# A two-layer mixer encoder on one core: where convolution's matmuls stand in the mixer, and behind what the weights at the stage joints are split

## The chip, the core and the metric

The kernel runs on one core of one Trainium2 chip. The metric is the device time of one execution in microseconds (us). A core has five engines, each with its own instruction stream: TensorE (PE) multiplies matrices, VectorE (DVE) and ScalarE (ACT) work elementwise, GpSimd (POOL) does a few small steps, SyncE (SP) issues most DMAs. An engine takes its instructions in the order in which they were put into its stream, and waits at the head of the stream until what the instruction needs is there. So the order of each stream, which is fixed when the kernel is built, decides what can hide what.

## What is computed

The reference is a two-layer encoder over 256 tokens of width 1024. Cut to what matters here:

```python
for l in range(DEPTH):                      # DEPTH = 2
    g = norm_g[l]
    h = rms_norm(x, g[0])
    x = x + 0.5 * rms_norm(swiglu(h, ffn_w_gate[l, 0], ffn_w_up[l, 0], ffn_w_down[l, 0]), g[1])
    h = rms_norm(x, g[2])
    z = h @ w_in[l]
    ...
    y = jnp.concatenate([y_conv, y_ret, y_rwkv, y_mlstm], axis=-1) @ w_out[l]
    x = x + rms_norm(y, g[3])
    h = rms_norm(x, g[4])
    x = x + 0.5 * rms_norm(swiglu(h, ffn_w_gate[l, 1], ffn_w_up[l, 1], ffn_w_down[l, 1]), g[5])
```

`swiglu(h, g, u, d)` is `(silu(h @ g) * (h @ u)) @ d` with 2816 inner columns. The four mixers are a short convolution, a retention scan, an RWKV-7 scan in both directions and an mLSTM, each 256 columns wide. All is float32.

## The kernel before, in words

**Stages.** The stages run in the order f00, m0, f01, f10, m1, f11: an FFN, the mixers and an FFN for each of the two layers (the digits of f are layer and place; m has the layer). There are four kinds of joints: FFN to mixer (f00 to m0, f10 to m1), mixer to FFN (m0 to f01, m1 to f11), FFN to FFN (f01 to f10), and the end behind f11.

**Weights.** All weights stream in elements of 128x1024 float32 (0.5 MB). `Stream.next` (L242 to L262) takes a raw tile from a pool of four, issues its DMA on SP's queue, then splits the element: ScalarE copies it to `hi` (rounded to the type that TensorE takes at full rate), VectorE subtracts to get `lo`. The first four elements of a stage are split in halves (`SPLITC`). Each product is made of three matmuls, hi by hi, hi by lo and lo by hi (`TERMS`). A raw tile comes free when its lo is done, and only then can the DMA of a later element that is given that tile start; SP issues its DMAs in order.

**An FFN** (`ffn`, L399). The 22 blocks `fb` of 128 inner columns need three elements each: a and b (gate and up, `fetch_ab`) and d (down, `fetch_d`). In the stream the order is a0 b0 a1 b1 a2 b2 d0 d1 d2, then a b d for each block; so element 6 is d0. `block` makes `pg` (L472, L474), the gating steps `gu`, and `hT` (hi on ScalarE, lo on VectorE at L488); `rows` makes the products `y` (L495) with the d element, for both token halves 0 and 1 (`tk`). For the last seven blocks (`NEPI`) the rows of token half 1 are kept back and stand behind all rows of token half 0, so that they cover the norm of token half 0: `resid` (`jk` squares on ScalarE, `yg`, `x` on VectorE) and `norm_t` (`jk`, `r_n` on POOL, `xg`, then `pt`, the transposes on TensorE at L314, and `XT`, the next stage's input, hi and lo). `turn()` emits the transposes and the XT writes.

**The mixers** (`mixers`, L560). The input projection gives z_in, q, k and v tiles; `conv` makes convolution's three projections, 6 elements, 24 matmuls of 128x256 each (`pz`, L388). The rwkv part is a generator: first it inverts small triangular blocks ("merge": 32x32 matmuls `pe`, L937 to L985), then runs the chain over chunks (`pakv`, `pu`, `psn`, `oT`, `pwc`), up to `pm` (L1065). mLSTM is a second generator (`pmb`, `pss`, `pom`). At the end stand 96 matmuls of the output projection (`ym`, L1334), in which two token halves take turns as in the FFN, and `ptf` (L786), the transposes of a mixer's output.

**What sets the order.** Each generator yields an estimate of the TensorE time of what it has just emitted. The loop at the end of `mixers` runs rwkv and, when the time of rwkv times a ratio is ahead of the time filled in, takes steps of the filler: `RATIO` with `fill1`, from "quads" (the merge) on `RATIO2` with `fill2`. Within `fill2`, `mix(a, b, R2)` puts convolution's steps between those of the retention output and mLSTM in the same way, and mLSTM's own estimate (`yield 0.22`) counts. A scheduler then places the instructions on the engines.

**Holds.** `held(*ins)` lets what is emitted inside stand on its engine only behind the instructions given, where they are on the same engine; it is an order, not a wait for another engine. `ffn` returns a table for the next stage, from element number to the instructions behind which its split stands: before, the elements 1 to 3 (2 and 3 ahead of a mixer) stood behind `done[1:]`, the lo half of the last `hT` on VectorE. `mixers` returned None, so the split of the next FFN's elements was free, and `fetch_ab` used `hold is None` to know that it follows a mixer.

Of the kernel before, what the change touches and what calls it, by code (L numbers as in the profile page):

```python
# [22 lines left out]
NFB = DFF // P  # L23
# [82 lines left out]
def tile_encoder(ctx: ExitStack, tc: tile.TileContext, x_in, wffn, win, wout, gains, params, idn, cst, rel, out, dbg=None):  # L106
# [286 lines left out]

    TA, TB, TC, SG = 4, 2, 7, 2
    NPRO, NEPI, SPLITC, WARM, W_FIN, ZW = 3, 7, 4, 6, 6.0, 2
    RATIO, RATIO2, W_PREP, W_INV, GRAIN, R1, R2, WQ, QG, KD = 0.8, 0.6, 8, 12, 0.8, 1.4, 1.2, 0.12, 8, 2

    def ffn(hold, l, j, XT, before1, before2, ahead, after, first, last, mix_next):

        st = Stream(wffn[l, j], f"f{l}{j}_", hold, first)  # L400
        ws, hts, nb = {}, {}, [0]

        def fetch_ab(fb):
            m = (m4, m4)
            new = m if fb == 2 or (fb == 1 and hold is None) else None
            ws[fb] = [st.next(new)]

            def second(ends=None):
                if ends:
                    st.hold[1] = ends  # L410
                ws[fb].append(st.next(new))
                return st.halves[0]

            if before1 and fb == 0:
                before1(second)
            else:
                second()
# [82 lines left out]
        turn = None  # L500
        hh = []
        for fb in range(NPRO):
# [4 lines left out]
            if fb == 0:  # L507
                turn = before2()
# [5 lines left out]
        y = ytiles(f"y{l}{j}")  # L514
# [26 lines left out]
        for fb in range(fb0, NFB - 4):  # L541
# [3 lines left out]
            if fb == fb0 + 3:  # L545
                mid = early + (st.dma,)
# [7 lines left out]

        for fb in range(NFB - 3, NFB):
            fetch_ab(fb)
            fetch_d(fb)
            done = block(fb)
        ahead(2)
        for fb in range(NFB - 4, NFB - 1):  # L560
            rows([fb], 0)
        end0 = rows([NFB - 1], 0)
        turn = after(0, y[0])
        with held(end0):
            for n, fb in enumerate(range(NFB - NEPI, NFB - SG)):
                rows([fb], 1)
                if n == TA and turn:
                    turn()
            rows(range(NFB - SG, NFB), 1)
        return y, {i: done[1:] for i in range(2 if mix_next else 1, 4)}, mid  # L570


    def split_out(dst, src_ps):
# [3 lines left out]
    def mixers(hold, l, XT, before2, ahead, after):  # L577
# [217 lines left out]
        hold = {}  # L795
# [365 lines left out]
        def mlstm():  # L1161
# [8 lines left out]
            for d in range(2):  # L1170
                for hp in range(2):
                    pm_ = ps.tile([P, 2, S], F32, tag="a", bufs=PA, name="pmb")
                    for i in range(2):
                        j = 4 * d + 2 * hp + i
                        T.matmul(pm_[:, i, :], lhsT=pair[64:128, j:j + 1].broadcast_to([64, P]), rhs=MR[64:128, d, :],
                                 start=i == 0, stop=True, skip_group_check=True)
                    yield 0.22
                    if d == 0 and hp == 0:
                        pc = ps.tile([P, 2, 16], F32, tag="o", bufs=1, name="pc")
                        for tk in range(2):  # L1180
                            T.matmul(pc[:, tk, :], lhsT=gT[:, tk * P:(tk + 1) * P], rhs=c_("sel"), start=tk == 0, stop=True,
                                     skip_group_check=True)
                        V.tensor_copy(out=cc, in_=pc[:, :, 0:8])
                        act(em, pc[:, :, 8:16], AF.Exp, scale=-1.0)
                    for i in range(2):
                        h = 2 * hp + i
                        j = 4 * d + h
                        for sk in range(2):
                            t0 = toff[d][sk]
                            act(wf[d][sk][:, h, :], pm_[:, i, t0:t0 + tn[d][sk]], AF.Exp, scale=-1.0,  # L1190
                                             bias=cc[:, sk, j:j + 1])
# [137 lines left out]
        y = [[], []]  # L1329
# [51 lines left out]
        for i in (4, 5):  # L1381
            for h in range(2):
                wo_rows(i, 1, h)
        turn()
        for h in range(2):
            for i in (6, 7):
                wo_rows(i, 1, h)
        return y, None


    seq = []
# [139 lines left out]
```

## Time and profile before

| what | us |
| --- | --- |
| median of three runs | 1164.4 |
| the three runs | 1164.4, 1154.44, 1165.07 |
| the profiled execution | 1157.71 |
| its span in the profile | 1156.0 |

The profile is of one execution; 1.71 us of it lie outside the span. In the rows that the prediction shows, a line of the timeline is start, duration, engine, line of the kernel, operation, output from input, shape and count; in square brackets stands how long the engine had been idle before it, and what released it. Matmuls are pipelined: a matmul of 128x512 is shown as 0.39 us long, but they start 0.23 us apart. The tables by stretch give the busy time of PE, PEld, DVE, ACT and POOL with the number of instructions, then the mean granted clock of TensorE (1.00 is full), the share of DMA time and GB/s.

### The profile page before, as it was taken

How to read it: one execution, taken by the hardware profiler on the slowest of the kernel's cores; microseconds unless marked ns; L12 is line 12 of the kernel's file. 1: busy time of each engine (PE TensorE's matmuls, PEld its weight loads, DVE VectorE, ACT ScalarE, POOL GpSimd, SP SyncE). 2: the span in 40 equal slices, each digit the busy share in tenths (PEclk: the TensorE clock that was granted, in tenths of full speed). 3: DMA queues.
4: the chain of work that ended last, by engine and by line, in shares of the span. 5: the costliest groups of instructions: out<-in, count | busy, mean ns of one | idle time of the engine just before them, and what ended most of it. 6: DMA issues, size and time to landing. Idle time of an engine off the chain costs nothing.

```text
span 1156.0 us, 20352 instructions
## 1 busy us (share of the span) xinstructions
PE 1116.3 (97%) x8083; PEld 954.3 (83%) x8083; DVE 787.4 (68%) x1371; ACT 653.5 (57%) x1193; POOL 51.4 (4%) x87
## 2 busy tenths in 40 slices
PE   8999999999899999999899999999989999999997
PEld 6888887897878788888798888879868778888886
DVE  6666566798867856566666656667895578566663
ACT  7575555777435755454555555568764157555562
POOL 0000000012000000000000000000301000000000
PEclk9999999999999999999999999999998799999999
DMA  7856554432323666655546655625242136665641
GB/s 259 278 188 202 181 189 157 145 125 90 114 72 108 202 222 193 203 174 199 179 149 207 215 186 186 209 73 185 74 159 63 56 127 205 204 196 185 197 163 37
DMA packets 53535, 189.46 MB, mean 164 GB/s; under 512 B 6200, under 2 KB 6848, under 8 KB 53440
## 3 DMA queue, kind: packets, MB, share of 16 engines
q1 hardware_dynamic: 51120, 181.28, 47.8%
q10 hardware_dynamic: 2320, 6.89, 1.8%
q8 instruction: 63, 1.03, 0.3%
q14 instruction: 32, 0.26, 0.1%
HBM read 187.10 MB, written 1.05 MB: 163 GB/s over the span
## 4 chain that ended last, share of the span: by engine, by line
PE 60%; DVE 12%; DMA 12%; ACT 8%; issue 6%; POOL 1%; SPq 0%; POOLq 0%; ACTq 0%; DVEq 0%
PE pg L472 16%; PE y L495 14%; DMA f_raw<-in_wffn_dram 11%; PE pz L388 9%; PE pg L474 8%; DVE f_lo L259 4%; ACT f_hi L142 4%; PE pgh L444 2%; DVE i_lo L259 1%; PE pss L1097 1%; PE pvg L594 1%; PE ym L1334 1%; ACT i_hi L142 1%; ACT jk L142 1%; DVE gu L121 1%
## 5 line engine op out<-in xcount | busy, mean ns | idle before, releaser
L259 DVE TENSOR_TENSOR f_lo<-f_raw,f_hi 128x1024 fp32r<-128x1024 f32 (+1 forms) x280 | 323.0, 1162 | 195.6 <-ACT f_hi L142 194.9
L472 PE MATMUL pg<-XT,f_hi 128*128 128x512 f32 x1232 | 387.4, 396 | 1.4 <-DVE gu L121 1.3
L142 ACT ACTIVATE f_hi<-f_raw 128x1024 fp32r<-128x1024 f32 (+1 forms) x280 | 279.0, 1007 | 137.8 <-DMA f_raw<-in_wffn_dram 116.6
L474 PEld LDWEIGHTS pg<-XT,f_lo 128*128 128x128 f32 x1232 | 231.3, 188 | 54.0
L474 PE MATMUL pg<-XT,f_lo 128*128 128x256 f32 x1232 | 242.2, 278 | 0.0
L495 PE MATMUL y<-f_hi,hT 128*128 128x512 f32 x704 | 232.6, 392 | 3.8 <-ACT hT L142 2.7
L472 PEld LDWEIGHTS pg<-XT,f_hi 128*128 128x128 f32 x1232 | 192.6, 189 | 7.4 <-DVE gu L121 2.2
L495 PEld LDWEIGHTS y<-f_hi,hT 128*128 128x128 f32 x704 | 131.6, 188 | 31.0 <-ACT hT L142 4.0
L388 PE MATMUL pz<-XT,i_hi 128*128 128x256 f32 x704 | 139.8, 295 | 2.2 <-DVE rvg L121 1.4
L495 PE MATMUL y<-f_lo,hT 128*128 128x512 f32 x352 | 137.3, 391 | 0.0
L388 PEld LDWEIGHTS pz<-XT,i_hi 128*128 128x128 f32 x704 | 111.4, 193 | 10.3 <-issue 4.1
L142 ACT ACTIVATE hT<-gu 128x256 fp32r<-128x256 f32 x77 | 32.1, 417 | 130.8 <-DVE gu L121 130.8
L388 PE MATMUL pz<-XT,i_lo 128*128 128x256 f32 x352 | 101.3, 288 | 0.0
L259 DVE TENSOR_TENSOR i_lo<-i_raw,i_hi 128x1024 fp32r<-128x1024 f32 (+1 forms) x68 | 73.6, 1095 | 14.5 <-ACT i_hi L142 13.5
L142 ACT ACTIVATE i_hi<-i_raw 128x1024 fp32r<-128x1024 f32 (+1 forms) x68 | 63.5, 953 | 34.4 <-PE pz L388 22.8
L121 DVE TENSOR_TENSOR gu<-pg,gu 128x256 f32<-128x256 f32 x154 | 64.4, 418 | 16.1 <-ACT gu L142 16.1
L495 PEld LDWEIGHTS y<-f_lo,hT 128*128 128x128 f32 x352 | 66.1, 188 | 11.1 <-DVE f_lo L259 0.4
L444 PE MATMUL pgh<-f_hi,XT 128*128 128x256 f32 x352 | 69.0, 290 | 2.1 <-ACT XT L142 1.1
L388 PEld LDWEIGHTS pz<-XT,i_lo 128*128 128x128 f32 x352 | 68.0, 193 | 0.8 <-issue 0.5
L142 ACT ACTIVATE gu<-pg 128x256 f32<-128x256 f32 x154 | 56.8, 369 | 18.7 <-PE pg L474 18.7
L444 PEld LDWEIGHTS pgh<-f_hi,XT 128*128 128x128 f32 x352 | 56.6, 191 | 5.3 <-ACT XT L142 1.8
L488 DVE TENSOR_TENSOR hT<-gu,hT 128x256 fp32r<-128x256 f32 x77 | 32.8, 425 | 35.1 <-ACT hT L142 34.5
(290 smaller groups left out, 1275.7 us busy)
## 6 DMA issues: line engine op xcount, KB each, us to landing
f_raw<-in_wffn_dram SPq DMA_DIRECT2D x262, 512.0 KB, 4.4
i_raw<-in_win_dram SPq DMA_DIRECT2D x60, 512.0 KB, 4.0
o_raw<-in_wout_dram SPq DMA_DIRECT2D x16, 512.0 KB, 3.7
gain<-in_gains_dram ACTq DMA_DIRECT2D x11, 512.0 KB, 4.9
x<-in_x_dram SPq DMA_DIRECT2D x4, 256.0 KB, 4.3
f_raw<-in_wffn_dram SPq DMA_DIRECT2D x4, 256.0 KB, 5.1
rl<-in_rel_dram ACTq DMA_DIRECT2D x2, 384.0 KB, 3.2
C<-in_cst_dram SPq DMA_DIRECT2D x1, 573.0 KB, 6.9
```

Of the source, the lines that this page charges most:

```text
L121: eng.tensor_tensor(out=out, in0=a, in1=b, op=op)
L142: return A.activation(out, a, f, **kw)
L259: V.tensor_tensor(out=lo[:, cs], in0=r[:, cs], in1=f(hi[:, cs]), op=ALU.subtract)))
L388: T.matmul(dst, lhsT=w[a][:, k * P:(k + 1) * P], rhs=xt(XT, k, b), start=n == 0, stop=n == 23)
L444: T.matmul(pg, lhsT=xt(XT, k, a)[:, tk * P:(tk + 1) * P], rhs=w[b][:, c:c + 256], start=n == 0, stop=n == 23)
L472: T.matmul(pg, lhsT=w[0][:, c:c + P], rhs=xt2(XT, k + i), start=k + i == 0, stop=False, skip_group_check=True)
L474: T.matmul(pg[:, 0, :], lhsT=w[1][:, c:c + P], rhs=xt(XT, k + i, 0), start=False, stop=k + i == 7, skip_group_check=True)
L488: V.tensor_tensor(out=hT[:, 1, :], in0=h, in1=f(hT[:, 0, :]), op=ALU.subtract))
L495: ins = T.matmul(y[tk][h], lhsT=hts[fb][:, a, tk * P:(tk + 1) * P], rhs=ws[fb][2][b][:, h * 512:(h + 1) * 512], start=fb == 0 and i == 0, ...
L594: T.matmul(pv[tk], lhsT=xt(XT, k, a)[:, tk * P:(tk + 1) * P], rhs=w[b][:, (k % 2) * 512:(k % 2 + 1) * 512], start=k == 0 and i == 0, stop= ...
L1097: T.matmul(pq[hp][:, p, :], lhsT=t[half[hp], 2 + p, sk * P:(sk + 1) * P], rhs=t[half[hp], p, :], start=p == 0, stop=True, skip_group_check ...
L1334: T.matmul(y[tk][h], lhsT=yT[(1, 0, 3, 2)[i // 2]][:, a, i % 2, tk * P:(tk + 1) * P], rhs=wo[i][b][:, h * 512:(h + 1) * 512], start=i == 0 ...
```

## The change

It has three parts.

1. Three numbers of the mixer's planner: `RATIO2` 0.6 to 0.75, `R2` 1.2 to 1.45, and mLSTM's yield from 0.22 to 0.5.
2. The last d element of each FFN is fetched and split behind the last block, held behind both halves of its `hT` (before it was fetched ahead of that block).
3. The holds at the joints. FFN to FFN: element 2 behind the last hT's lo, elements 3 and 4 behind `ends`, the last XT writes of token half 0 (`turn()` now hands them out). FFN to mixer: elements 2 and 3 as before. Mixer to FFN, free before: element 2 behind the two steps that scale `xg`, element 3 behind `ends`. The key "mix" takes the place of the test for None.

```diff
@@ -393,7 +393,7 @@
 
     TA, TB, TC, SG = 4, 2, 7, 2
     NPRO, NEPI, SPLITC, WARM, W_FIN, ZW = 3, 7, 4, 6, 6.0, 2
-    RATIO, RATIO2, W_PREP, W_INV, GRAIN, R1, R2, WQ, QG, KD = 0.8, 0.6, 8, 12, 0.8, 1.4, 1.2, 0.12, 8, 2
+    RATIO, RATIO2, W_PREP, W_INV, GRAIN, R1, R2, WQ, QG, KD = 0.8, 0.75, 8, 12, 0.8, 1.4, 1.45, 0.12, 8, 2
 
     def ffn(hold, l, j, XT, before1, before2, ahead, after, first, last, mix_next):
 
@@ -402,7 +402,7 @@
 
         def fetch_ab(fb):
             m = (m4, m4)
-            new = m if fb == 2 or (fb == 1 and hold is None) else None
+            new = m if fb == 2 or (fb == 1 and "mix" in hold) else None
             ws[fb] = [st.next(new)]
 
             def second(ends=None):
@@ -554,8 +554,12 @@
 
         for fb in range(NFB - 3, NFB):
             fetch_ab(fb)
-            fetch_d(fb)
+            if fb < NFB - 1:
+                fetch_d(fb)
             done = block(fb)
+
+        st.hold[st.i] = done
+        fetch_d(NFB - 1)
         ahead(2)
         for fb in range(NFB - 4, NFB - 1):
             rows([fb], 0)
@@ -565,9 +569,9 @@
             for n, fb in enumerate(range(NFB - NEPI, NFB - SG)):
                 rows([fb], 1)
                 if n == TA and turn:
-                    turn()
+                    r = turn()
             rows(range(NFB - SG, NFB), 1)
-        return y, {i: done[1:] for i in range(2 if mix_next else 1, 4)}, mid
+        return y, {2: done[1:], 3: done[1:] if mix_next or last else r[1], 4: () if mix_next or last else r[1]}, mid
 
 
     def split_out(dst, src_ps):
@@ -1174,7 +1178,7 @@
                         j = 4 * d + 2 * hp + i
                         T.matmul(pm_[:, i, :], lhsT=pair[64:128, j:j + 1].broadcast_to([64, P]), rhs=MR[64:128, d, :],
                                  start=i == 0, stop=True, skip_group_check=True)
-                    yield 0.22
+                    yield 0.5
                     if d == 0 and hp == 0:
                         pc = ps.tile([P, 2, 16], F32, tag="o", bufs=1, name="pc")
                         for tk in range(2):
@@ -1381,11 +1385,12 @@
         for i in (4, 5):
             for h in range(2):
                 wo_rows(i, 1, h)
-        turn()
+        r = turn()
         for h in range(2):
             for i in (6, 7):
                 wo_rows(i, 1, h)
-        return y, None
+
+        return y, {"mix": True, 2: r[0], 3: r[1]}
 
 
     seq = []
```

What it does to the order is not seen in the diff. Three places, as the rows stand on an engine; a name's number at its end tells one tile from another, and behind f00_, i0_, o0_ stand the stage's stream, hi, lo or raw, and the element's number.

ScalarE at the joint f00 to m0, before (hT_1830 is the last block's hT, i0 the mixer's stream, jk the first step of the norm):

```order
L142 ACTIVATE gu_1826<-pg_1809 128x256
L142 ACTIVATE hT_1830<-gu_1805 128x256
L142 ACTIVATE i0_hi3_1992<-i0_raw3_1990 128x512 x2
L142 ACTIVATE jk_1862,st3_1861<-y00_00_317 128x512
L142 ACTIVATE jk_1864,st3_1861<-y00_01_318 128x512
```

and after (f00_hi65 is the last d element):

```order
L142 ACTIVATE gu_1820<-pg_1803 128x256
L142 ACTIVATE hT_1824<-gu_1799 128x256
L142 ACTIVATE f00_hi65_1829<-f00_raw65_1827 128x1024
L142 ACTIVATE i0_hi3_1992<-i0_raw3_1990 128x512 x2
L142 ACTIVATE jk_1862,st3_1861<-y00_00_317 128x512
```

The last d element's copy moved in between the last hT and the norm. On VectorE its lo moved in the same way, between the lo halves of the mixer's elements 2 and 3:

```order
L488 TENSOR_TENSOR hT_1824<-gu_1799,hT_1824 128x256
L259 TENSOR_TENSOR i0_lo2_1985<-i0_raw2_1982,i0_hi2_1984 128x512 x2
L259 TENSOR_TENSOR f00_lo65_1830<-f00_raw65_1827,f00_hi65_1829 128x1024
L259 TENSOR_TENSOR i0_lo3_1993<-i0_raw3_1990,i0_hi3_1992 128x512 x2
L121 TENSOR_TENSOR yg_1866<-y00_00_317,gain0_1_671 128x512
```

VectorE at the joint f01 to f10, ahead of the norm's first step yg, before:

```order
L488 TENSOR_TENSOR hT_5972<-gu_5947,hT_5972 128x256
L259 TENSOR_TENSOR f10_lo1_6100<-f10_raw1_6097,f10_hi1_6099 128x512 x2
L259 TENSOR_TENSOR f10_lo2_6163<-f10_raw2_6160,f10_hi2_6162 128x512 x2
L259 TENSOR_TENSOR f10_lo3_6171<-f10_raw3_6168,f10_hi3_6170 128x512 x2
L121 TENSOR_TENSOR yg_6008<-y01_00_4472,gain0_5_4888 128x512
```

and after:

```order
L488 TENSOR_TENSOR hT_5966<-gu_5941,hT_5966 128x256
L259 TENSOR_TENSOR f10_lo2_6163<-f10_raw2_6160,f10_hi2_6162 128x512 x2
L259 TENSOR_TENSOR f01_lo65_5972<-f01_raw65_5969,f01_hi65_5971 128x1024
L121 TENSOR_TENSOR yg_6008<-y01_00_4472,gain0_5_4888 128x512
L139 SCALAR_TENSOR_TENSOR st3_6003<-st3_6003 128x1
```

Elements 1 and 3 left the place ahead of yg, and f01's last d element came to stand there.

TensorE between the merge and the chain in m0, before (pe5 is the merge's last step, pakv the chain's first, pmb and pc are mLSTM's, pz is convolution's):

```order
L997 MATMUL pakv_3526<-UV0_2624,GP01_2530 64x64
L388 MATMUL pz_3495<-XT0_21_1834,i0_lo26_3499 128x256
L388 MATMUL pz_3495<-XT0_21_1834,i0_hi26_3498 128x256 x2
L985 MATMUL pe5_3415<-D64T_3191,F__3413 32x32 x31
L388 MATMUL pz_3495<-XT0_21_1834,i0_lo26_3499 128x256
L997 MATMUL pakv_3526<-UV0_2624,GP00_2516 64x64
L1175 MATMUL pmb_3490<-MR_3405,pair_85 128x256 x2
```

and after:

```order
L388 MATMUL pz_3551<-XT0_20_1833,i0_hi27_3554 128x256
L1179 MATMUL pmb_3478<-MR_3432,pair_85 128x256 x2
L1179 MATMUL pmb_3490<-MR_3432,pair_85 128x256 x2
L388 MATMUL pz_3551<-XT0_20_1833,i0_hi27_3554 128x256
L388 MATMUL pz_3551<-XT0_20_1833,i0_lo27_3555 128x256
L1001 MATMUL pakv_3535<-UV0_2624,GP00_2516 64x64
L1001 MATMUL pakv_3535<-UV0_2624,GP01_2530 64x64
```

The four pz next to pe5 x31 moved forward: six pz now stand ahead of pe5's first row (not shown) and six (three, one and two) between it and these last rows; behind them come pakv, pc, pe5 x31 and pmb without a pz, then six pz.

## The prediction

> **What bounds the kernel now.** I read the page's busy times first, then a table by stage with the granted clock, then the timeline of TensorE for its idle times, then the other engines' rows beside those.
>
> The first line of the page (engine, busy us, share, instructions):
>
> ```profile
> PE 1116.3 (97%) x8083; PEld 954.3 (83%) x8083; DVE 787.4 (68%) x1371; ACT 653.5 (57%) x1193; POOL 51.4 (4%) x87
> ```
>
> TensorE is busy 1116.3 of 1156.0 us. No edit takes a matmul away, so the change can only move the 40 us in which TensorE is not busy, or the clock at which it is. The same work of the two mixers, the end of the merge and the rwkv chain, in stretches (PE, PEld, DVE, ACT, POOL busy; then the granted clock):
>
> ```profile
> 311.00:350.50 39.50, 39.50 (x645) 32.02 (x639) 25.03 (x63) 14.76 (x41) 2.59 (x6) 1.00 0.27 82
> 876.10:927.20 51.10, 51.10 (x642) 40.06 (x638) 25.90 (x64) 14.84 (x42) 2.46 (x4) 0.73 0.22 64
> 882.50:885.00 2.50, 2.50 (x73) 2.06 (x71) 1.23 (x1) 2.48 (x9) 0.00 (x0) 1.00 0.23 26
> 885.00:887.50 2.50, 2.50 (x32) 2.18 (x31) 0.69 (x1) 1.81 (x6) 1.23 (x2) 0.53 0.51 190
> 887.50:910.00 22.50, 22.50 (x152) 15.62 (x150) 7.91 (x21) 4.29 (x11) 1.23 (x2) 0.50 0.00 1
> 910.00:912.50 2.50, 2.50 (x19) 2.05 (x16) 1.61 (x4) 0.07 (x1) 0.00 (x0) 0.51 0.02 7
> 912.50:915.00 2.50, 2.50 (x60) 2.23 (x62) 1.89 (x6) 0.64 (x3) 0.00 (x0) 1.00 0.00 0
> ```
>
> Layer 0 takes 39.5 us, layer 1 51.1 us for as many matmuls. From 885 to 912.4 the clock is at half, and that costs 51.1 − 39.5 = 11.6 us. It is the largest thing here that the change can touch: the runs lie between 1154.4 and 1165.1, which is about one such stretch apart. What stands ahead of the drop, in layer 0 at full clock:
>
> ```profile
> 314.56 0.40 PE L388 MATMUL pz<-XT,i_hi 128*128 128x256 f32 x2
> ...
> 316.58 0.62 PE L1181 MATMUL pc<-C,gA 128*128 128x16 f32 x4
> ...
> 317.50 0.38 PE L388 MATMUL pz<-XT,i_lo 128*128 128x256 f32 x1
> 317.72 0.40 PE L388 MATMUL pz<-XT,i_hi 128*128 128x256 f32 x2
> 318.05 1.19 PE L985 MATMUL pe<-D64T,F__3413 32*32 32x32 f32 x62
> 319.17 0.38 PE L388 MATMUL pz<-XT,i_lo 128*128 128x256 f32 x1
> ...
> 319.74 0.50 PE L1175 MATMUL pmb<-MR,pair 64*128 64x256 f32 x2
> 320.17 1.03 PE L997 MATMUL pakv<-UV,GP 64*64 64x64 f32 x28
> ...
> 322.04 0.51 PE L388 MATMUL pz<-XT,i_hi 128*128 128x256 f32 x2
> ```
>
> Layer 1's clock drops where layer 0 is at about 319.9. From 314.96, the end of the first row, to 322.04, 7.1 us, only four of convolution's 128x256 matmuls run (pz); most of the rest are 32x32 and 64x64 pieces.
>
> **The change part by part.**
>
> *Convolution spread (RATIO2, R2, 0.5).* The same 144 matmuls move from behind pm to between the merge's and the chain's. By the order, six pz now stand ahead of pe5's first row, six more among the first pakv and pmb, then comes one stretch with none: 20 rows of pakv (two matmuls each, 40 at 1.03/28 = 0.037, 1.5 us), pc (0.6), pe5 (318.05 to 319.17, 1.1) and one pmb row (319.74 to 320.17, 0.4), together 3.6 us, then 6 pz and soon 14. With four pz allowed as before, the thin stretch is some 5 us long in place of 7.1 (two pmb rows, four of pakv and four pz more). So a drop becomes rarer, not impossible. I take the value without a drop, −11.6 us against the profiled run, and keep 0 as the other end. The merge's own waits:
>
> ```profile
> 301.06 0.25 PE L949 MATMUL pe<-En,DT 32*32 32x32 f32 x5 [0.42 <-DVE En L943]
> 302.01 0.37 PE L949 MATMUL pe<-En,DT 32*32 32x32 f32 x22 [0.70 <-issue]
> ...
> 868.40 0.38 PE L949 MATMUL pe<-En,DT 32*32 32x32 f32 x21 [0.74 <-issue]
> ```
>
> More pz in front of pe cover a wait for VectorE; what "issue" is, no row shows. Of 0.42 + 0.70 + 0.74 = 1.9 I take half, −0.9 (bounds −1.9 and 0). The 36 pz that stood behind pm covered the end of the chain; now ym stands there, 96 matmuls at 0.23, 22 us, and its weights stand ahead of it on ScalarE and VectorE. I cost that at nothing; were o's first weights late, pm's tail would show.
>
> *Last d element behind the last block, before a mixer.* The place in the timelines:
>
> ```profile
> 179.05 0.50 PE L472 MATMUL pg<-XT,f_hi 128*128 128x512 f32 x1 [0.77 <-DVE gu L121]
> 177.58 1.04 ACT L142 ACTIVATE f_hi<-f_raw 128x1024 fp32r<-128x1024 f32 x1
> 178.92 1.22 DVE L259 TENSOR_TENSOR f_lo<-f_raw,f_hi 128x1024 fp32r<-128x1024 f32 x1
> 188.93 0.42 ACT L142 ACTIVATE hT<-gu 128x256 fp32r<-128x256 f32 x1 [0.95 <-DVE gu L121]
> 189.38 0.43 DVE L488 TENSOR_TENSOR hT<-gu,hT 128x256 fp32r<-128x256 f32 x1 [0.48 <-ACT hT L142]
> 189.72 2.49 DVE L259 TENSOR_TENSOR i_lo<-i_raw,i_hi 128x512 fp32r<-128x512 f32 x4
> 189.40 0.50 PE L495 MATMUL y<-f_hi,hT 128*128 128x512 f32 x1 [0.40 <-ACT hT L142]
> 197.69 1.03 PE L314 MATMUL pt<-ident,xg 128*128 128x128 f32 x8
> 755.39 0.50 PE L495 MATMUL y<-f_hi,hT 128*128 128x512 f32 x1 [0.40 <-ACT hT L142]
> ```
>
> Early, one hi (1.04) and one lo (1.22) go from in front of gu, so the 0.77 wait at 179.05 goes and hT comes at about 188.6 in place of 189.35. Late, the last six y of token half 0 need the element. ScalarE copies it behind hT (to 189.6). VectorE does hT lo (0.34), the two halves of the next stage's element 2 (half of 2.49, 1.25) and then f_lo (1.22), done at 188.6 + 0.34 + 1.25 + 1.22 = 191.4. Four of the six y wait for that and take 0.9, so they end at 192.3; before, six from 189.40 at 0.23 each end at 190.8. That is +1.6 us. Layer 1 has no 0.77 to win: +2.3. Behind f_lo on VectorE stand element 3's lo and yg, behind f_hi on ScalarE element 3's hi and jk: about 1.2 us later each, but pt at 197.69 moves with TensorE by 1.6, so the norm is no new wait. Element 3's DMA no longer reuses the last ab slot but the one of the next stage's element 0, whose lo stands eleven rows earlier on VectorE; I take it as in time. Sum +3.9 (bounds 0, if VectorE's backlog in the mixer swallows it, and +4.6).
>
> *The same at the end of the last FFN.* Nothing of a next stage stands between:
>
> ```profile
> 1136.04 0.42 ACT L142 ACTIVATE hT<-gu 128x256 fp32r<-128x256 f32 x1 [0.95 <-DVE gu L121]
> 1139.41 0.60 ACT L142 ACTIVATE jk<-y 128x512 bf16<-128x512 f32 x1 [2.96 <-PE y L495]
> ```
>
> The last six y end at 1139.4, so they begin at 1138.0 and the first lo among them at 1138.2; f_lo is done at 1136.46 + 1.05 + 1.22 = 1138.7. +0.5 (0 to 1.2).
>
> *FFN to FFN.*
>
> ```profile
> 562.12 1.06 ACT L142 ACTIVATE f_hi<-f_raw 128x1024 fp32r<-128x1024 f32 x1 [1.63 <-DMA f_raw<-in_wffn_dram]
> 565.26 0.42 ACT L142 ACTIVATE hT<-gu 128x256 fp32r<-128x256 f32 x1 [1.81 <-DVE gu L121]
> 566.05 3.69 DVE L259 TENSOR_TENSOR f_lo<-f_raw,f_hi 128x512 fp32r<-128x512 f32 x6
> 565.73 0.50 PE L495 MATMUL y<-f_hi,hT 128*128 128x512 f32 x1 [1.94 <-ACT hT L142]
> 576.04 0.41 PE L314 MATMUL pt<-ident,xg 128*128 128x128 f32 x2 [1.85 <-DVE xg L301]
> ```
>
> Element 4's copy no longer holds up the last gu for its DMA, so hT comes about 2 us earlier; then the d element's lo takes as long as the 1.94 did. Of the six half lo (3.69) ahead of yg two stay, with one whole lo (1.22), all 2 us earlier: the norm gains about 2, and pt's 1.85 goes. But elements 3 and 4 are now split behind the turn, and the second half of element 3's lo stands on VectorE behind the other token half's whole norm; TensorE reaches it about 1.5 us too early. Sum 0 (−1.9 to +1.9).
>
> *Mixer to FFN, twice.*
>
> ```profile
> 363.73 0.44 PE L786 MATMUL ptf<-ident,og 128*128 128x128 f32 x2 [1.15 <-DVE og L121]
> 383.14 0.33 PE L314 MATMUL pt<-ident,xg 128*128 128x128 f32 x1 [1.75 <-DVE xg L301]
> 396.08 0.49 PE L495 MATMUL y<-f_hi,hT 128*128 128x512 f32 x1 [0.78 <-ACT f_hi L142]
> ...
> f_raw<-in_wffn_dram SPq DMA_DIRECT2D x262, 512.0 KB, 4.4
> ```
>
> ptf now stands behind more than 36 ym, which cover its 1.15. pt moves behind all ym, the halves of elements 2 to 4 go from in front of it on VectorE, and its wait stays near 1.7. Element 2 now waits for the scaled xg, so its slot comes free later, and d0, whose DMA waits for that slot (4.4 us to land), makes the 0.78 about 2.2; element 3's late half adds some 0.75. −1.15 + 1.4 + 0.75 = +1.0 each, +2.0 (bounds −2.3, nothing late, and +7.2, a landing uncovered each time: 4.4 − 0.78).
>
> *Sum* against the profiled execution's 1157.7: −0.9 + 3.9 + 0.5 + 0 + 2.0 = +5.5, 1163.2 with one half-clock stretch as in that execution; −11.6 without, **1151.6**. The profiled execution is 6.7 below the median of the runs, 1164.4, as if that median had more of the half clock.
>
> [...] In the rows above, TensorE is busy 2.50 of 2.50 us just ahead of the drop, and the half clock lasts 27.4 us. [...]
>
> **The rivals.**
> 1. *The drop stays in one layer*: the 3.6 us without any pz are longer than a gap of before, such as 319.55 to 322.04. Against it: twelve pz stand closely ahead, six behind. 1163.2.
> 2. *It comes in both layers*, as the median above hints: 1163.2 + 11.6 = 1174.8.
> 3. *The joints do what they are changed for* and nothing is late: all terms at their good bounds, no drop: 1157.7 − 11.6 − 1.9 + 0 + 0 − 1.9 − 2.3 = 1140.0. Against it: the reuse of slots and the order.
> 4. *Slower*: the half clock, once entered, is kept to the end of the chain in each layer, since pz come in ones to fives there and a dense stretch comes only with ym. The 27.4 us at half cost 11.6, so they held 15.8 us of work: 0.73 us for each. From 319.9 to pm at 350.5 are 30.6 us of work, 22.5 us a layer: 1151.6 + 45 = 1196.6. It decides if no stretch of the chain is dense enough to bring the clock back. Against it: layer 1 came back within such a chain.
>
> **How the numbers follow.** No drop 0.46 (1151.6; its own range, 1145 to 1157, takes some half of each term's bounds); one layer 0.34; both 0.09; the joints' gain 0.07; slower 0.04. The likeliest is 1151.6. The range, 1143 to 1170, takes in the first two cases with their bounds and leaves out 0.20. Within 1% of 1164.4 (1152.8 to 1176.0), about what a measurement of this kernel can tell from no change, lie a part of the first case, nearly all of the second and most of the third. Faster: 0.6 of 0.46, 0.07, and 0.05 for runs that lie below the profiled one as 1154.4 did, 0.40; slower: 0.04 and 0.4 of 0.09, 0.08; within, 0.52.
>
> **What would show it.** Granted clock 1.00 in both layers from the merge to pm; about 39 us for that stretch. Idle of 2 to 3 us at the last y of token half 0 in both FFNs before a mixer, released by f_lo; none at pt there. No 1.94 from a late hT between the FFNs and no 1.85 at pt, but a wait for f_lo twice. No wait at ptf; a longer one for d0. I am wrong if the clock still drops, if y behind hT does not wait for f_lo, or if TensorE waits for d0 to d2 by more than 3 us.

## The result and the profile after

| what | before | after |
| --- | --- | --- |
| median, us (20 runs each, same chip, in turn) | 1155.09 | 1161.01 |
| lowest and highest, us | 1150.32, 1180.05 | 1156.9, 1172.03 |
| ratio after to before, 95% interval | | 1.0066, 1.0044 to 1.0088 |
| the profiled execution, us | 1157.71 | 1163.84 |
| its span, us; its mean granted clock | 1156.0; 0.988 | 1162.1; 0.988 |

The change costs 0.66% by the ratio, which compares fast runs only; the medians of all runs lie 5.9 us apart, 0.51%. That lies within the 1% that the prediction called no change, but the interval leaves 1.0 out, so it is a small loss. 1151.6 was forecast, inside a range of 1143 to 1170. The measured time lies in the range, but on the other side of before: a gain was forecast, and it is a loss.

The first line of the page of after (engine, busy us, share of the span, instructions):

```profile
PE 1119.2 (96%) x8083; PEld 955.8 (82%) x8083; DVE 787.0 (68%) x1371; ACT 648.3 (56%) x1193; POOL 50.9 (4%) x87
```

TensorE has the same 8083 matmuls and is busy 2.9 us longer; the other 3.2 us of the longer span are idle time. The end of a mixer, in three stretches: from the merge's first pe to the first pm, from there to the first ym, from there to the first pgh of the next FFN. First layer 0 of before, then layer 0 and layer 1 of after (busy time of PE, PEld, DVE, ACT, POOL with the number of instructions, then granted clock, DMA share, GB/s):

```profile
297.97:350.48 52.51, 50.79 (x1073) 42.18 (x1073) 36.41 (x81) 19.98 (x49) 4.25 (x7) 1.00 0.29 89
350.48:359.19 8.71, 8.71 (x96) 8.06 (x95) 5.16 (x14) 5.50 (x12) 0.11 (x1) 1.00 0.01 3
359.19:385.91 26.72, 23.82 (x110) 18.95 (x109) 22.42 (x39) 16.87 (x33) 3.65 (x5) 1.00 0.52 169
```

```profile
300.63:356.16 55.53, 54.48 (x1101) 45.37 (x1101) 36.45 (x79) 19.91 (x50) 4.36 (x7) 1.00 0.27 85
356.16:360.17 4.01, 4.01 (x50) 3.58 (x50) 2.89 (x6) 2.41 (x5) 0.00 (x0) 1.00 0.01 2
360.17:389.64 29.47, 25.47 (x127) 19.82 (x125) 22.19 (x44) 17.25 (x35) 3.42 (x7) 0.99 0.43 143
869.80:930.94 61.14, 59.88 (x1102) 50.09 (x1102) 36.76 (x80) 20.18 (x50) 4.29 (x5) 0.89 0.25 77
930.94:934.94 4.00, 4.00 (x50) 3.57 (x49) 2.69 (x6) 2.40 (x5) 0.00 (x0) 1.00 0.00 0
934.94:964.99 30.05, 25.96 (x127) 20.47 (x125) 22.23 (x44) 17.36 (x36) 3.67 (x4) 0.96 0.43 140
```

The reader should compare layer 0's rows in order. The first stretch holds 28 matmuls more by the records and is 3.0 us longer; the second is 4.7 us shorter; the third, which holds the output projection and the norm, is 2.8 us longer, and in it TensorE is idle 29.47 − 25.47 = 4.00 us where before it was idle 2.90. So work was moved ahead of pm, pm came later by it, and what stands behind pm did not get shorter by as much.

The waits of TensorE in after at the places the prediction spoke of (start, duration, engine, line, operation, output from input, and in brackets the idle time and its releaser):

```profile
191.50 0.50 PE L495 MATMUL y<-f_lo,hT 128*128 128x512 f32 x1 [1.12 <-DVE f_lo L259]
371.85 0.66 PE L790 MATMUL ptf<-ident,og 128*128 128x128 f32 x4 [1.15 <-DVE og L121]
388.51 1.35 PE L314 MATMUL pt<-ident,xg 128*128 128x128 f32 x8 [2.85 <-DVE xg L301]
397.51 0.73 PE L495 MATMUL y<-f_hi,hT 128*128 128x512 f32 x2 [1.31 <-ACT f_hi L142]
569.50 0.50 PE L495 MATMUL y<-f_lo,hT 128*128 128x512 f32 x1 [0.99 <-DVE f_lo L259]
760.56 0.51 PE L495 MATMUL y<-f_lo,hT 128*128 128x512 f32 x1 [1.12 <-DVE f_lo L259]
963.37 0.90 PE L314 MATMUL pt<-ident,xg 128*128 128x128 f32 x3 [2.93 <-DVE xg L301]
973.50 0.73 PE L495 MATMUL y<-f_hi,hT 128*128 128x512 f32 x2 [1.31 <-ACT f_hi L142]
```

The waits for f_lo came as forecast, smaller. The wait for ptf did not go, and the one for pt, which was to stay near 1.7, is 2.85 and 2.93.

The granted clock in after, at the four places ahead of the program's last 2 us where it was not full:

```profile
390.00:392.50 2.50, 2.50 (x13) 2.50 (x13) 2.41 (x6) 1.54 (x6) 0.15 (x1) 0.50 0.08 15
...
847.50:850.00 2.50, 2.50 (x7) 1.98 (x6) 2.48 (x7) 2.50 (x4) 0.00 (x0) 0.50 0.61 202
...
892.50:902.50 10.00, 10.00 (x122) 8.45 (x121) 4.38 (x9) 5.37 (x18) 1.41 (x2) 0.50 0.18 54
...
962.50:965.00 2.50, 1.63 (x9) 1.61 (x9) 0.71 (x3) 1.78 (x6) 0.83 (x2) 0.53 0.00 0
965.00:967.50 2.50, 2.50 (x14) 2.50 (x12) 2.40 (x6) 1.53 (x5) 0.00 (x1) 0.50 0.00 0
```

Worked out from the mean clock of these and the partly affected stretches beside them, the half clock lasts 3.4, 3.4, 13.7 and 6.8 us, 27.3 in all: as much as in the profiled execution of before, but half of it in the chain of layer 1, and 10.2 us at the joints from mixer to FFN, at the longer wait for pt. Of the three signs of being wrong that the prediction named, the first came (the clock still drops) and the other two did not: y waits for f_lo, and the waits for d0, 1.31, stay below 3 us.

### The profile page after: what moved, and what is told of

Same layout as the page of the kernel before. It is cut to its first block, busy times and chain, and to the rows that moved or that the text cites. A ratio compares the mean times of both kernels' runs of the same rounds, so it can differ in the third digit from the quotient of the medians.

```text
span 1162.1 us, 20338 instructions
## 1 busy us (share of the span) xinstructions
PE 1119.2 (96%) x8083; PEld 955.8 (82%) x8083; DVE 787.0 (68%) x1371; ACT 648.3 (56%) x1193; POOL 50.9 (4%) x87
## 3 DMA queue, kind: packets, MB, share of 16 engines
HBM read 187.10 MB, written 1.05 MB: 162 GB/s over the span
## 4 chain that ended last, share of the span: by engine, by line
PE 65%; DVE 13%; DMA 8%; ACT 7%; issue 5%; POOL 1%; POOLq 0%; DVEq 0%; ACTq 0%; SPq 0%
PE pg L472 18%; PE y L495 15%; PE pz L388 9%; PE pg L474 9%; DMA f_raw<-in_wffn_dram 8%; DVE f_lo L259 4%; PE pgh L444 4%; ACT f_hi L142 2%; DVE i_lo L259 2%; PE pvg L598 1%; ACT i_hi L142 1%; DVE gu L121 1%; PE pss L1101 1%; PE pt L314 1%; DVE xg L121 1%
```

## The experiments

All times are ratios to the kernel before, run in turn on the same chip; times in us are the ratio's difference times the median of before in the same series (1152.3, 1153.6 and 1153.4). "pe to pgh" is the length of the three stretches above, for layer 0 and layer 1.

### A second profile of before

> The kernel before once more, for its trace on this chip. All theories: the stages as in the profile shown, the FFNs within 2 us of it; the half clock somewhere in the second mixer or nowhere.

It took 1155.34. In the chain of layer 1 its clock was at half for 6.8 us in place of 27.3, and for 3.4 us twice in the mixers' input. Pe to pgh: 87.8 and 89.4 (87.9 and 98.2 in the profile shown, where layer 1 has the long stretch). FFN f10 took 2.4 us longer than in the profile shown (190.1 in place of 187.7), more than the 2 us expected. TensorE waited for gu in both layers:

```profile
180.16 0.73 PE L472 MATMUL pg<-XT,f_hi 128*128 128x512 f32 x2 [1.08 <-DVE gu L121]
750.39 0.72 PE L472 MATMUL pg<-XT,f_hi 128*128 128x512 f32 x2 [1.04 <-DVE gu L121]
```

So the long half-clock stretch, from which the prediction started, isn't as long in each execution. And the wait for gu, which the prediction found in layer 0 alone, can stand in both.

### The parts, one at a time

Convolution's three numbers alone:

```diff
-    RATIO, RATIO2, W_PREP, W_INV, GRAIN, R1, R2, WQ, QG, KD = 0.8, 0.6, 8, 12, 0.8, 1.4, 1.2, 0.12, 8, 2
+    RATIO, RATIO2, W_PREP, W_INV, GRAIN, R1, R2, WQ, QG, KD = 0.8, 0.75, 8, 12, 0.8, 1.4, 1.45, 0.12, 8, 2
-                    yield 0.22
+                    yield 0.5
```

> Convolution's three numbers alone. Theory A (the clock follows how thickly TensorE is filled): the merge's waits shrink by about 1.7 us a layer and the half-clock stretch in layer 1's chain is 13.7 us long in place of 27.3, which saves 5 us more: 5 to 8 us faster than before, no half clock at the joints. Rival B (the half clock comes by chance, whatever the order): 1 to 3 us faster, half-clock time on average as in before.

The last d element alone:

```diff
-            fetch_d(fb)
+            if fb < NFB - 1:
+                fetch_d(fb)
...
+        st.hold[st.i] = done
+        fetch_d(NFB - 1)
```

> The last d element behind the last block alone. Theory A: +1.6 and +2.3 us at the two FFN-to-mixer joints, +0.5 at the end, 0 to +1 between the FFNs: 4 to 5 us slower, with waits of about 1.1 us for f_lo at the last y of token half 0. Rival B (the early gu wait that goes pays for it): within 1 us of before.

The holds from FFN to FFN alone:

```diff
-                    turn()
+                    r = turn()
-        return y, {i: done[1:] for i in range(2 if mix_next else 1, 4)}, mid
+        return y, {2: done[1:], 3: done[1:] if mix_next or last else r[1], 4: () if mix_next or last else r[1]}, mid
```

> The holds between the FFNs alone. Theory A: the waits for hT (1.94) and for pt (1.85) there go, and little comes back: 2.5 to 4 us faster. Rival B (my prediction's term): what is won comes back at the late halves of element 3, 0 within 1 us.

The holds from mixer to FFN alone:

```diff
-            new = m if fb == 2 or (fb == 1 and hold is None) else None
+            new = m if fb == 2 or (fb == 1 and "mix" in hold) else None
-        turn()
+        r = turn()
-        return y, None
+        return y, {"mix": True, 2: r[0], 3: r[1]}
```

> The holds between mixer and FFN alone. Theory A: pt waits about 2.9 us at each of the two joints, TensorE is thinly used there, the clock goes to half for 3.4 to 6.8 us behind pt in each layer: 6 to 9 us slower. Rival B (my prediction's term): +1 us a joint without a clock change, 2 us slower in all.

And two together, the last d element and the holds from FFN to FFN:

> The last d element behind the last block and the holds between the FFNs, without the other two parts. Theory A (both parts remove the same two waits between the FFNs, for hT and for pt, some 4 us once): about 4 us faster than before, like the last d element alone. Rival B (their gains add up): 6 us faster or more.

| part | ratio, 95% interval | us | pe to pgh |
| --- | --- | --- | --- |
| convolution | 1.0092, 1.0061 to 1.0123 | +10.6 | 92.0, 91.4 |
| last d | 0.9966, 0.9930 to 1.0002 | −3.9 | 87.5, 87.3 |
| FFN to FFN | 1.0007, 0.9974 to 1.0040 | +0.8 | 87.8, 89.8 |
| mixer to FFN | 1.0036, 1.0004 to 1.0067 | +4.1 | 87.7, 86.1 |
| last d and FFN to FFN | 0.9990, 0.9952 to 1.0027 | −1.2 | 91.0, 87.8 |

For convolution both theories had a gain, and neither held. The last d element came out faster, where a loss of 4 to 5 us or no change was expected, but its interval just reaches 0. The holds from FFN to FFN came out at rival B's 0, those from mixer to FFN between the two theories. The two parts together fall short of either theory's gain, with an interval (−5.5 to +3.1 us) that takes in the 4 us of theory A.

Convolution's spread is the part that costs. Of its 10.6 us some 4 in each layer lie between pe and pgh; where the other 2 to 3 lie is not shown. Layer 0 with convolution's numbers alone, and its waits for ptf and pt, then pt's in layer 1:

```profile
299.26:355.95 56.69, 54.48 (x1102) 45.36 (x1102) 36.45 (x79) 19.95 (x50) 4.38 (x7) 1.00 0.27 83
355.95:359.95 4.00, 4.00 (x50) 3.57 (x49) 2.89 (x6) 2.41 (x5) 0.00 (x0) 1.00 0.00 2
359.95:391.23 31.28, 26.33 (x127) 20.45 (x125) 24.87 (x48) 20.22 (x41) 4.63 (x7) 0.95 0.46 151
```

```profile
371.63 0.66 PE L786 MATMUL ptf<-ident,og 128*128 128x128 f32 x4 [1.13 <-DVE og L121]
389.20 1.97 PE L314 MATMUL pt<-ident,xg 128*128 128x128 f32 x8 [3.76 <-DVE xg L301]
962.12 1.97 PE L314 MATMUL pt<-ident,xg 128*128 128x128 f32 x8 [4.26 <-DVE xg L301]
```

From pm to pgh it is 35.3 us, as before (35.4): a chain over og (the gated output of a mixer), ptf, the last ym of token half 0, the norm and pt, which TensorE's work has to cover. Of convolution's 144 matmuls, 36 stood behind pm before and 5 do now. The 31 that are gone take 31 × 0.12 = 3.7 us (in the profile of before, nine of convolution's matmuls start between 306.05 and 307.13, 0.12 us apart); pm comes 4.2 us later (56.69 from pe in place of 52.51), and the stage with it. In the order of TensorE, ym of token half 1 now fill the place ahead of ptf, and 17 of them are left behind token half 0's last ym, in place of 28 and 8 more behind pt: that is where the wait for pt comes from.

The 35.3 us are not made up as before, though. ptf comes 15.68 us behind pm in place of 13.25 (363.73 − 350.48), because og on VectorE comes later. VectorE in layer 0, before:

```profile
359.16 0.69 DVE L121 TENSOR_TENSOR og<-og,hsum 128x512 f32<-128x512 f32 x1
360.36 0.42 DVE L121 TENSOR_TENSOR up<-pz,cc 128x256 f32<-128x256 f32 x1
```

and with convolution's numbers alone:

```profile
357.79 0.42 DVE L121 TENSOR_TENSOR up<-pz,cc 128x256 f32<-128x256 f32 x1
362.59 0.42 DVE L121 TENSOR_TENSOR yT<-yc,yT 128x256 fp32r<-128x256 f32 x1
366.19 0.69 DVE L259 TENSOR_TENSOR o_lo<-o_raw,o_hi 128x512 fp32r<-128x512 f32 x1
366.79 0.69 DVE L121 TENSOR_TENSOR og<-og,hsum 128x512 f32<-128x512 f32 x1
```

With its matmuls done earlier, convolution's steps on VectorE (up, four yc, a yT, 2.6 us) came to stand between pm and og, and so did two halves of o_lo (1.4 us); before, they stood behind og. og starts 10.84 us behind pm in place of 8.68. The place of ptf is the same in both layers and in every run of an order: 15.7 us behind pm with 5 of convolution's matmuls left there, 13.25 with 36, 12.2 with 45. The stage did not get longer by this as well, since fewer ym stand between ptf and pgh. So a later pm and a later og came with the spread together; what each costs by itself no run separates.

With the last d element alone the waits at the joint f01 to f10 are gone, the ones before the mixers are 1.12 for f_lo at either place, and the wait for gu is gone in exchange. The holds from mixer to FFN alone bring a wait at each joint, for the lo of element 3, whose split they put behind the turn:

```profile
395.10 0.38 PE L444 MATMUL pgh<-f_lo,XT 128*128 128x256 f32 x1 [1.31 <-DVE f_lo L259]
959.96 0.39 PE L444 MATMUL pgh<-f_lo,XT 128*128 128x256 f32 x1 [1.31 <-DVE f_lo L259]
```

It takes the place of the wait for d0 (0.78 before, in layer 0), so it accounts for a part of the 4.1 us; the rest is not seen in a row.

### The whole change without convolution's numbers

> The changed kernel without convolution's two numbers: last d behind the last block and behind the steps of the norm, all three joints, convolution as before. Theory (convolution's spread carries the whole loss, by about 4 us a layer, and the joints give a little at one and take 1.3 us at each joint from mixer to feed-forward): pe to pgh 87 to 88.5 us a layer, ratio to before 0.996 to 1.001, so 6 to 9 us under the changed kernel's. Rival (the holds at the joints carry the loss too): ratio 1.003 to 1.006 with pe to pgh near 88.

0.9987 (0.9958 to 1.0017), −1.5 us; pe to pgh 87.2 and 86.7. The last d element and the holds together cost nothing that can be measured; the loss of the change goes with convolution's numbers, and does not need the joints.

### Convolution's numbers with more work kept behind

The ym of token half 1 held behind token half 0's last, with convolution's numbers:

```diff
-                wo_rows(i, 0, h)
+                last0 = wo_rows(i, 0, h)
...
-                wo_rows(i, 1, h)
+                with held(last0):
+                    wo_rows(i, 1, h)
```

> Convolution's three numbers, with the ym of token half 1 from the third element on held behind the last ym of token half 0, so that 36 of them follow it again in place of 17. Theory A (the chain behind pm is late, whatever stands behind): TensorE waits ahead of the last ym of token half 0 instead of at pt; within 2 us of convolution's numbers alone, still 8 us or more slower than before. Rival C (the chain is not late, its end has only lost its cover): pt's wait of 3.8 us shrinks below 2, the half clock at the joints goes, 5 us or more faster than convolution's numbers alone.

1.0062 (1.0028 to 1.0096), +7.2 us; one of its runs took 2152.3 us, which stands alone and for which no cause was found. Pe to pgh 91.5 and 91.8. The waits of layer 0:

```profile
372.25 0.66 PE L786 MATMUL ptf<-ident,og 128*128 128x128 f32 x4 [1.50 <-DVE og L121]
374.42 0.73 PE L1334 MATMUL ym<-o_hi,yT 128*128 128x512 f32 x2 [1.51 <-ACT o_hi L142]
389.77 1.09 PE L314 MATMUL pt<-ident,xg 128*128 128x128 f32 x8 [0.87 <-DVE xg L301]
```

The wait for pt fell from 3.76 to 0.87, and 1.51 came at o_hi and 0.37 at ptf in its place. Half clock came there too (3.4 and 6.8 us, ahead of the norm in place of behind it). So each theory held in part: the wait at pt shrank as C said, and the time stayed within 3.4 us of convolution's numbers alone, with overlapping intervals, near what A said. Where the ym stand decides where TensorE waits; the wait itself stays for the most part (4.4 us idle from ym to pgh in layer 0, in place of 5.0), as pm and og come as late as before this edit.

### Less ahead of pm

Only the chain's rate, the other way: 45 of convolution's matmuls behind pm.

```diff
-    ... R1, R2, ... = ... 1.4, 1.2, ...
+    ... R1, R2, ... = ... 1.4, 1.0, ...
```

> The kernel before with R2 at 1.0 in place of 1.2: convolution's matmuls are taken later, 45 of them behind pm in place of 36 (5 in the changed kernel). Theory A (the mixer ends a fixed time behind pm, because og, ptf, the last ym of token half 0 and the norm follow one another, so what delays pm delays the stage): pm comes 1 us earlier, the 1.15 us at ptf go, 1 to 3 us faster than before. Rival B (convolution's numbers cost by the clock alone): same within 1 us, unless the half clock changes.

0.9945 (0.9913 to 0.9978), −6.3 us; pe to pgh 86.6 and 86.7. Layer 0:

```profile
302.11:353.87 51.76, 49.94 (x1069) 41.66 (x1070) 34.99 (x79) 18.27 (x46) 4.25 (x7) 1.00 0.26 81
353.87:363.32 9.45, 9.45 (x99) 8.83 (x98) 7.01 (x17) 7.78 (x17) 0.11 (x1) 1.00 0.20 58
363.32:388.73 25.41, 23.69 (x110) 18.96 (x109) 21.59 (x38) 16.34 (x31) 3.28 (x5) 1.00 0.55 179
```

The first stretch is shorter, the second longer, and the third is idle for 1.7 us where before it was idle for 2.9. The wait for ptf shrank from 1.15 to 0.77 and did not go. Up to pgh it is 1.3 us less in layer 0; more is won behind it, up to the first whole block of f01. Its first pg in layer 0, before and here:

```profile
411.99 0.70 PE L472 MATMUL pg<-XT,f_hi 128*128 128x512 f32 x2
```

```profile
412.55 0.71 PE L472 MATMUL pg<-XT,f_hi 128*128 128x512 f32 x2
```

From pe to there it is 114.0 us before (411.99 − 297.97) and 110.4 here (412.55 − 302.11), 110.7 in layer 1: 3.6 us less, and in layer 0 the waits of before for d0 (0.78) and for a half block's hh (0.86), both behind pt, are gone. With convolution's numbers alone it is 118.0 and 117.5. So most of the 6.3 us lies between pe and the first pg; the FFNs behind it are not read, since two profiles of before differ there by more than 2 us (f10 takes 187.7 in the one and 190.1 in the other).

The same with the last d element behind the last block:

> The kernel before with two edits: the chain's rate number 1.0 in place of 1.2 (45 of convolution's matmuls behind pm in place of 36), and the last d element's cast behind the last block in the feed-forward stages. Alone they measured 0.9945 and 0.9966 of before. Theory (the two act at different places, the end of the mixer and the joint between feed-forward stages): their gains add, ratio 0.988 to 0.994, and in the profile the stretch from the first pe to the next stage's first pgh stays near 86.7 us a layer (87.8 before), with the waits for hT and pt at the joint f01 to f10 gone (194.6 us for f01 becomes about 189.5). Rival (each of them moved the time only by its share of half clock): ratio 0.995 to 1.000, with the stretches as before.

**0.9897** (0.9858 to 0.9936), 1142.8 us, 10.6 under the median of before: the fastest of all, and faster than both kernels. The two gains add (0.9945 × 0.9966 = 0.991). Pe to pgh is 87.2 and 86.9 us, and f01 takes 187.7 us, without the waits for hT and pt at its end, about as the theory had it. All six of its runs lie between 1141.9 and 1144.9.

And with the merge's rate lowered too (RATIO2 0.5, R2 1.0, last d), 56 matmuls behind pm:

> As the run before last, with the merge's rate number lowered too (0.5 in place of 0.6): 56 of convolution's matmuls behind pm. Theory (convolution ahead of pm delays pm, and pm sets the end as long as the latency chain behind it is longer than the work that covers it): with 45 behind pm the wait for ptf had already gone, so the cover is now the longer and no more is won: within 0.3% of the run with 45, pe to pgh 86 to 88 us a layer. Rival (earlier pm always helps): 84 to 85 us a layer, another 4 us off. A third: the chain is thinned, half clock appears between pe and pm and it is 3 to 8 us slower.

0.9930 (0.9901 to 0.9958). The median is 4.3 us above that of the run with 45, a little more than the 0.3% expected; the intervals overlap, so more is not shown to be worse, but it isn't better. In layer 1 of the profiled execution the chain has a half-clock stretch of 27.3 us. In layer 0, at full clock, TensorE is idle 3.2 us from pe to pm (1.8 with 45) and 3.2 from the first ym to pgh, 89.1 from pe to pgh. Convolution's matmuls are now missing as filler ahead of pm; and ptf comes 15.05 us behind pm, in place of 12.2 with 45, so the wait for ptf, 0.77 with 45 and not gone there, is 1.22 again.

### Filling the wait at the joint

Convolution's numbers alone, with twelve more matmuls, whose output nothing reads, between the last ym and pt (`turn()` moves behind them):

```diff
+        spare = ps.tile([P, 512], F32, tag="o", bufs=1, name="spare")
+        with held(ins):
+            for n in range(12):
+                ins = T.matmul(spare, lhsT=yT[0][:, 0, 0, 0:P], rhs=wo[7][0][:, 0:512], start=True, stop=True)
+        with held(ins):
+            turn()
```

> The kernel before with convolution's numbers alone (as in the run that measured 1.0092 of before), and 12 spare matmuls of 128x512 (0.23 us each, 2.7 us in all, into a PSUM tile that nothing reads) between the last ym and pt at each joint from mixer to feed-forward, where TensorE waited 3.8 and 4.3 us. It tells whether the half clock at these joints follows from that wait. Theory (it does): the half-clock stretches there (387 to 397 us and 960 to 970 us in the profile with convolution's numbers alone) are gone, the wait ahead of pt is about 1.2 us, and the time is 2 to 6 us under that run's 1162.9, though still above before, since the chain from og over the norm to pt still ends as late. Rival (the half clock comes from something else, such as the load ahead of it): half-clock stretches at the joints remain, and the time stays at 1161 to 1165 us.

1.0080 (1.0046 to 1.0113): as slow as without them, within the intervals. Of the theory one half held and the other fell. The joint of layer 1 with convolution's numbers alone, then filled:

```profile
957.50:960.00 2.50, 0.36 (x2) 0.00 (x0) 2.42 (x5) 2.10 (x6) 0.30 (x1) 1.00 0.48 187
960.00:962.50 2.50, 0.38 (x2) 0.39 (x3) 2.04 (x5) 1.77 (x6) 0.94 (x1) 0.85 0.20 25
962.50:965.00 2.50, 2.44 (x12) 2.04 (x10) 2.07 (x5) 2.50 (x5) 0.87 (x1) 0.50 0.71 211
965.00:967.50 2.50, 2.40 (x11) 2.10 (x11) 2.50 (x6) 0.96 (x4) 0.00 (x0) 0.50 0.72 220
```

```profile
960.00:962.50 2.50, 1.31 (x9) 0.86 (x8) 1.81 (x5) 1.80 (x6) 0.83 (x2) 1.00 0.40 93
962.50:965.00 2.50, 1.05 (x6) 0.85 (x7) 2.32 (x4) 2.10 (x5) 0.79 (x1) 1.00 0.69 205
```

Filled, both joints stay at full clock in the profile, with waits of 1.46 and 1.12 at pt in place of 3.76 and 4.26: there the half clock went with the longer wait. But it costs next to nothing at this place. The first pg of f01, with convolution's numbers alone and filled, with pt ahead of each:

```profile
389.20 1.97 PE L314 MATMUL pt<-ident,xg 128*128 128x128 f32 x8 [3.76 <-DVE xg L301]
417.22 0.70 PE L472 MATMUL pg<-XT,f_hi 128*128 128x512 f32 x2
```

```profile
390.38 1.09 PE L314 MATMUL pt<-ident,xg 128*128 128x128 f32 x8 [1.46 <-DVE xg L301]
418.38 0.70 PE L472 MATMUL pg<-XT,f_hi 128*128 128x512 f32 x2
```

It comes 28.02 and 28.00 us behind pt (28.11 and 27.97 in layer 1): with half the clock over the first 6 us and with all of it. Filled, TensorE has short waits there (0.93 at the first pgh of layer 1) that slower matmuls take up. So the loss is not in the clock. Taken over runs: the four filled ones whose mean granted clock was 0.995 or more took 1162.0 on average, the fourteen of before on the same chip 1151.3.

## Why the prediction was wrong, point by point

**The clock, −11.6: the term that made the forecast 1151.6, and it failed.** Half clock in the chain was to go; in the profiled execution of after 13.7 us of it are there in layer 1 (a mean clock of 0.89 from pe to pm), and 27 us in all. Two things were wrong. The price was taken from one execution as if every one paid it: the second profile of before had 6.8 us of it, and in the three series of experiments the runs of before had median clocks of 0.993 to 0.996, against 0.988 in the profile shown. The median of three runs that the prediction had, 1164.4, is 1155.09 over twenty. A typical execution had less than 11.6 to win. And whether the spread makes the stretch rarer is not shown: between the first pe and the first ym, half clock is there in one of eight mixers with the spread (after, and the runs with convolution alone, held and filled), and in five of twenty without it. In after it began 21.2 us behind the first pe, and in both profiles of before 21.1: at the place that the prediction looked at, where few of convolution's matmuls run. The rival "the drop stays in one layer" gave 1163.2; the profiled execution took 1163.84, but with a drop half as long and a loss elsewhere, which is the next point; that the numbers are close is luck.

**Convolution from behind pm, "I cost that at nothing": the step that carries the loss.** The prediction said that ym would cover the end of the chain in its place. Ym did move there, and were then missing where they had covered the norm. Alone this part measured +10.6 us, some 4 of them in each mixer: pm comes 4.2 us later in layer 0, og comes another 2 us later behind pm, since convolution's steps on VectorE moved ahead of it, and TensorE, with less left to do, waits for pt by 3.76 and 4.26 in place of 1.75 and 1.29. The filled run shows that the loss is there at full clock, and the series 5, 36 and 45 matmuls behind pm that it goes with their number (92, 88 and 87 us from pe to pgh), up to a point: with 56 it is 89. That the spread is the cause is shown by taking it alone and by leaving it out; how the loss divides between the later pm and the later og is not.

**The merge's waits, −0.9.** From pe to pm TensorE was idle 1.7 us in layer 0 before and 1.05 after; with convolution's numbers alone 2.2. No gain that can be told from the scatter.

**Last d ahead of a mixer, +3.9, and at the end, +0.5.** Alone it measured −3.9, with an interval that just reaches 0. The forecast wait for f_lo was there, but 1.12 long, where 2 to 3 us were forecast, and a wait for gu (1.08 and 1.04 in the second profile of before) went in exchange, of which the prediction had 0.77 in one layer. That makes about 0; the gain came at the joint from FFN to FFN. At the end of f11 no wait is seen.

**FFN to FFN, 0.** The two waits, 1.94 and 1.85, went, as forecast; one for f_lo of 0.99 came, where two were forecast. But last d alone removes the same two, so with it the holds had nothing left to win: −3.9 alone, −1.2 with them, the intervals overlapping. The holds alone measured +0.8, with an interval of −3.0 to +4.6: f01 is 189.6 us long there in place of 193.8 and 194.6, f10 191.2 in place of 187.7 and 190.1. So the 0 came out, but that it comes back at the late half of element 3, as the prediction had it, is not shown: no wait of TensorE for that element above 0.15 us stands in the profile.

**Mixer to FFN, +2.0.** Alone +4.1 (0.5 to 7.7). Alone, the wait is 1.31 at each joint for the lo of element 3, where 0.75 was forecast, and there is none for d0. In the whole change it is for d0, 1.31 at each joint, where 2.2 was forecast, by the mechanism that was forecast: element 2 is split later, and d0's DMA, which takes its slot, starts at 391.46, 2.95 us behind pt, in place of 383.75, 0.6 behind pt. The wait for ptf stayed, against the forecast: ptf does stand behind 39 ym, but og comes 2.2 us later behind pm. In the whole change these holds also gave something back: from pm to pgh it is 33.5 and 34.1 us, in place of 35.3 and 35.8 with convolution alone, and VectorE has 44 instructions in place of 48 in that last stretch of layer 0. That is the likely reason why the whole change comes out below convolution alone (1.0066 and 1.0092, with overlapping intervals); it was not tried by itself.

**The sum.** Without the clock term the prediction had +5.5, and the medians differ by +5.9. That is chance: convolution was at −0.9 and is at +10.6, the rest of the change was at +6.4 and is at −1.5.

What stays open: which of convolution's numbers, the merge's or the chain's, costs more was not tried, and the cause of the long half-clock stretch in the chain was not found; in the 15 us ahead of it TensorE is busy throughout in before, and has one wait of 0.54 us in after.

## What to carry to other kernels

Work that needs nothing is worth most behind the last result of a latency chain: before spreading it evenly, count what is left to cover the steps that follow, down to the next stage's first matmul, and look at which of its steps on other engines move ahead of that chain's with it. Moving the remaining work about then only moves the wait. A price that one profiled execution shows (a clock stretch above all) is to be weighed by how many executions have it, before it is put into a sum.

## What the runs showed of the hardware

The half clock comes in pieces: 3.4, 3.4, 13.7 and 6.8 us in after, 27.3 in before. Within 0.1 us they are 1, 1, 4, 2 and 8 times 3.4 (27.3 / 8 = 3.41), and so are those in the profiles of the experiments (3.4, 6.8 or 27.3 each), with 27.3 once more in the chain of the run with 56, but for a rest at the end (1.2 us in before, 1.5 in after). At the joints from mixer to FFN it followed waits: 3.76 and 4.26 us at pt came with 6.8 us of half clock each, 2.85 and 2.93 with 3.4 and 6.8, 1.75 and 1.29 in before with none, and 1.46 and 1.12 at the filled joints with none. The length of one wait does not decide it, though: 1.31 with the holds from mixer to FFN alone came with 3.4 in layer 0 and with none in layer 1.

The price of the half clock was not the same in two places: 11.6 us for 27.3 in the chain of layer 1 in before, where TensorE is busy without a gap (51.10 of 51.10 us), and nothing that can be seen at the joint (28.02 us from pt to the first pg with it and 28.00 without in layer 0, 28.11 and 27.97 in layer 1), where the next FFN has waits of its own to fill.

Matmuls on the rounded type of hi and lo took TensorE less time than float32 ones of the same shape: mLSTM's pmb of 64x256, on the rounded type, start 0.16 us apart (in before, four of them from 315.32 to 315.97), its pss of 64x256, on float32, 0.27 (four from 323.43 to 324.49).
